# Pools at multiples of 2048 bytes, earlier modulation sums and later sums of activations in a two-layer encoder

## The chip, the cores and the metric

The kernel runs on one core of one Trainium2 chip. The metric is the device time of one launch in microseconds, as the median of several runs. The core has five engines with a queue of instructions each: TensorE (PE, matmuls; PEld is its weight loads), VectorE (DVE), ScalarE (ACT), GpSimd (POOL) and SyncE (SP, which issues the transfers). They wait for each other by semaphores. On-chip memory has 128 partitions; an address below is a byte offset within a partition.

## The reference, cut to what matters

A trunk of two layers works on 256 tokens of 2048 features in float32. Each layer has an attention part (two kinds of heads with one input and one output projection) and an MLP; a conditioning vector gives six vectors per layer that scale, shift and gate.

```
cond = silu(c)
for l in range(2):
    mod = cond @ w_ada[l] + b_ada[l]                 # 2048 x 12288
    sh_a, sc_a, g_a, sh_m, sc_m, g_m = split(mod, 6)
    h = rmsnorm(x) * (1 + sc_a) + sh_a
    proj = h @ w_in[l]
    ...                                              # differential and latent attention
    x = x + g_a * (concat([out_a, out_b]) @ w_o[l])
    h = rmsnorm(x) * (1 + sc_m) + sh_m
    y = square(relu(h @ w_mlp_in[l])) @ w_mlp_out[l] # 2048 -> 8192 -> 2048
    x = x + g_m * y
return rmsnorm(x, final_norm_g)
```

## The kernel before

Every float32 operand is split in two parts: ACT rounds it (hi, line 157), DVE subtracts to get the rest (lo, line 160), and PE forms hi·hi, hi·lo and lo·hi. A weight block of 1 MB arrives in a tile `raw` of a ring of five (pool wp, which also holds hi and lo); the same ring takes the blocks of w_ada. A modulation value costs one DVE instruction over 128x2048 (line 313, `ada`), one per block; each weight split adds a rate (RATE_A0 and so on) to a credit, and a credit of one loads the next block of w_ada, whose sum is put behind that split's last lo.

Layer 2's MLP (`mlp_last`) is the place of most of the change. The hidden features go in 32 pairs of 128-row blocks. `wides` multiplies two weight blocks by the normalized h into one bank: 16 matmuls of 512 columns (line 222, hi), then 16 of 256 columns (line 225, lo). `hidden` makes relu squared of a pair, its parts hidh and hidl (line 1390 is the DVE half), four sums of its quarters (lines 1100 to 1102, `sum4`) and the parts sumh and suml of these. The first three pairs were computed ahead, during the output projection; `leave` (that is `scaled`, line 657) takes them from their banks when the MLP begins. For the second matrix product a step either takes eight products of blocks (`eight`, operands hi and lo) or seven products with sums of weight blocks (`seven_weights`: u is formed by DVE on lines 1128 to 1130, parts dh, dl of the raw blocks and uh, ul of the sums on lines 1138 and 1139). `product` (lines 1147 to 1149) is three matmuls of 512 columns whose moving operand is the weight part. A seven-step is 9 matmuls on d and 12 on u; its third product reads the sums (sumh, suml), as do three of those on u. 42 of the 56 steps are seven-steps: 30 of them in the first half of the output (28 in the loop over pairs, two behind it) and 12 in the second, where the hidden parts are fetched back from memory (`back`).

In the loop pair j is computed while step j - 4 is multiplied. PE's order there is written out by hand: wides, products 1, 2, 3 (on d), wides, products 5, 7, 6, 4 (on u). Below, A to I are the wides in turn from the MLP's start, and S0, S1, S2 the first three seven-steps: PE's order is A, B, C, first products of S0, D, rest of S0, E, first products of S1, F, rest of S1, G, first products of S2, H, and so on. The order on DVE, ACT and SP comes from a scheduler, which has only the program and its own costs.

Pools are laid out one behind the other. In this kernel the tiles of the pools wp (hi, lo, raw, u), up and tp begin 512 bytes past a multiple of 2048, x 416 past one, and the last pools, kp among them (dh, dl, uh, ul), 1376 past one, which is 32 past a multiple of 64. dh, dl, uh, ul have one buffer each.

Of the kernel before, what the change touches and what calls it, by code (L numbers as in the profile page):

```python
# [10 lines left out]
F32 = mybir.dt.float32  # L11
F32R = mybir.dt.float32r
# [5 lines left out]
P = 128  # L18
T = 256
TX = T + 2  # L20
D = 2048
NK = D // P
# [31 lines left out]
V_LAM = 208  # L54
V_T = 216
V_C = 248
NVEC = 264


def two_pi_parts():  # L60
# [35 lines left out]
NAHEAD = 6  # L96
# [6 lines left out]

LATE = 2
TURNED = 0, 0, 2
RATE_A0, RATE_Q, RATE_A3, RATE_O, RATE_A1, RATE_A2, RATE_K, RATE_M, RATE_V = 0.7, 2.7, 1.7, 0.75, 0.5, 0.7, 0.6, 0.68, 1.15
FILL = "0|1|2|3|e|l||r"


class Trunk:  # L110
    def __init__(self, ctx, tc, io):
        self.nc, self.tc, self.io = tc.nc, tc, io
        pool = lambda name, bufs, **k: ctx.enter_context(tc.tile_pool(name=name, bufs=bufs, **k))
        self.fp = pool("fp", 1)
        self.wp = pool("wp", 4)
        self.up = pool("up", 40)
        self.tp = pool("tp", 6)
        self.cp = pool("cp", 1)
        self.sp = pool("sp", 8)
        self.pp = pool("pp", 8, space=bass.MemoryType.PSUM)  # L120
        self.late = ctx.enter_context(ExitStack())
        self.lp = self.late.enter_context(tc.tile_pool(name="lp", bufs=1))
        self.ap = self.late.enter_context(tc.tile_pool(name="ap", bufs=6))
        self.ada_todo, self.ada_here, self.rate, self.credit = [], [], 0.0, 0.0
        self.n = 0
        self.rt = []
        self.evict = None
        self.most = None
        self.hold = None
# [159 lines left out]
    def ada_plan(self):  # L289
        self.mod, self.macc = {}, {}  # L290
        for l in range(DEPTH):
            for g in range(6):
                self.mod[l, g] = self.cp.tile([P, NK], F32, name=f"mod{l}{g}")
                self.macc[l, g] = (self.cp if l else self.fp).tile([P, NK], F32, name=f"macc{l}{g}")
        for l in range(DEPTH):
            for gs in ((0, 1), (2,), (3, 4), (5,)):
                self.ada_todo += [(l, g, 2 * q + i) for q in range(8) for g in gs for i in range(2)]
        self.ada_todo.remove(TURNED)
# [55 lines left out]
    def setup(self):  # L354
        nc, io, cp = self.nc, self.io, self.cp
        self.ada_plan()
        self.cond = self.lp.tile([P, D], F32, name="cond")
        row = self.wp.tile([1, D], F32, tag="raw", name="c_row", bufs=5)
        nc.sync.dma_start(row, io["c"])
        tab = cp.tile([P, T + 8 + NCONST + NVEC], F32, name="tab")  # L360
        nc.scalar.dma_start(tab, io["tab"])
        self.pos = tab[:, : T + 8].bitcast(I32)
        self.K = tab[:, T + 8 : T + 8 + NCONST]
        self.vec = tab[:, T + 8 + NCONST :]
        self.x = cp.tile([P, NK, T], F32, name="x")
        for q in range(4):
            nc.sync.dma_start(self.x[:, 4 * q : 4 * q + 4], io["xT"][:, 4 * q : 4 * q + 4])
        self.mean = {}
        for n in (D, 2 * P):
            self.mean[n] = cp.tile([P, P], F32, name=f"mean{n}")  # L370
            nc.gpsimd.memset(self.mean[n], 1.0 / n)
        self.eps = cp.tile([P, 1], F32, name="eps")
        nc.gpsimd.memset(self.eps, EPS)
        self.ident = cp.tile([P, P], F32, name="ident")
        make_identity(nc, self.ident)
        self.ccol = cp.tile([P, NK], F32, name="ccol")
        self.lead = nc.scalar.activation(self.s("warm", 1), self.eps, AF.Silu)
        leads = []
        for j in range(4):
            c = slice(512 * j, 512 * j + 512)  # L380
            ps = self.bank("pc").rearrange("p a b -> p (a b)")
            nc.tensor.matmul(ps, self.mean[D][:1], row[:, c], start=True, stop=True)
            self.lead = nc.scalar.activation(self.cond[:, c], ps, AF.Silu, scale=float(D))
            leads.append(self.lead)
            if j == 0:
                self.bias_setup()
        nc.scalar.activation(self.ccol, self.vec[:, V_C : V_C + NK], AF.Silu)
        self.rel = {0: self.distances(0)}
        ps = self.bank("pn")[:, 0]
        for k in range(0, NK, 2):  # L390
            t = self.t("sqx")
            last = nc.scalar.activation(t, self.x[:, k : k + 2], AF.Square)  # L392
            self.follow(last, leads[min(3, 1 + k // 4)])
            for i in range(2):
                nc.tensor.matmul(ps, self.mean[D], t[:, i], start=k + i == 0, stop=k + i == NK - 1)
        self.follow(nc.scalar.activation(self.s("warm", 1), self.eps, AF.Sqrt), last)
        r = self.cp.tile([P, T], F32, tag="rstd", name="rstd", bufs=2)
        nc.scalar.activation(r, ps, AF.Sqrt, bias=self.eps)
        return r
# [6 lines left out]
    def lambdas(self):  # L406
        nc = self.nc
        e = self.s("lam_e", 4)
        v = self.vec[:, V_LAM : V_LAM + 8]
        nc.vector.tensor_tensor(v[:, :4], v[:, :4], v[:, 4:], ALU.mult)  # L410
        ps = self.bank("pl")[:, 0, :4]
        nc.tensor.matmul(ps, self.mean[D], v[:, :4], start=True, stop=True)
        nc.scalar.activation(e, ps, AF.Exp, scale=float(D))
        self.lam = self.cp.tile([P, 2], F32, name="lam")
        self.gl = self.cp.tile([P, 2, 2], F32, name="gl")
        for l in range(2):
            init = 0.8 - 0.6 * math.exp(-0.3 * l)
            nc.vector.scalar_tensor_tensor(
                self.lam[:, l : l + 1], e[:, 2 * l : 2 * l + 1], init, e[:, 2 * l + 1 : 2 * l + 2],
                ALU.add, ALU.subtract,  # L420
            )
            nc.vector.tensor_scalar(
                self.gl[:, l], self.vec[:, V_SUBLN + 2 * l : V_SUBLN + 2 * l + 2], 1.0 - init, None, ALU.mult
            )
# [319 lines left out]
    def layer(self, l, acc, st):  # L744
        nc, io = self.nc, self.io
# [12 lines left out]
        if l == 0:  # L758
            early = {p: next_by_k(kqs) for p, kqs in EARLY.items()}
# [4 lines left out]
        else:  # L764
            h = acc
            lat = []
            for b in range(0, NAHEAD, 2):
                t, c = self.scaled(st, b, self.u("cr"))
# [164 lines left out]
        with self.tc.manual_schedule(engines={mybir.EngineType.PE}) if l else nullcontext():  # L933
# [19 lines left out]
            self.rate = 0.0 if st else RATE_K  # L953
            if st:
                h = self.ahead_rest(st, 0, acc, 2, 5)
                first = NAHEAD, lambda: [self.scaled(st, b, self.t("sum")) for b in range(0, NAHEAD, 2)]
            else:
                h, banks = self.norm_then_by_k(l, acc, 3, 4, io["w_n0"], 3, 0)
                high = self.high
                first = NNORM, lambda: [  # L960
                    self.relu2(b, after=a) for b, a in zip(banks, [high, *self.highs, *self.highs[1:] * 3])
                ]
# [52 lines left out]
    def mlp_last(self, l, h, first, g):  # L1015
# [8 lines left out]
        lead = done // 2  # L1024
        banks = None

        def both(j, v, bias=None):
            hid[j], part[j] = self.hidden(v, bias)
            kept[j] = self.spill(hid[j], f"a{j}")
            if j in sevens:  # L1030
                kept[j] += self.spill(part[j], f"s{j}")

        for j in range(lead, NPAIR):
            pre = [self.t("pre") for _ in range(2)]
            step = j - LAG
            for i in range(2):
                (ps,) = self.wides([io["w_m1"][l, 2 * j + i - done]], h)
                if j == lead and i == 0:
                    for k, (v, c) in enumerate(leave()):
                        both(k, v, c)  # L1040
                for k in range(2):
                    self.nc.scalar.activation(pre[k][:, i], ps[:, k], AF.Copy)  # L1042
                if i:
                    self.nc.vector.tensor_tensor(pre[0], pre[0], pre[1], ALU.add)
                    both(j, pre[0])
                if step < 0:
                    continue
                if i == 0:
                    banks = banks or {p: self.flat(self.bank("p7")) for p in ORDER}
                    w = self.seven_weights(io["w_s"][0, step])  # L1050
                self.products(banks, ORDER[3:] if i else ORDER[:3], w, hid[step], part[step], step == 0)
# [16 lines left out]
        hid = []  # L1068
# [19 lines left out]
    def hidden(self, v, bias=None):  # L1088
# [6 lines left out]
            for i in range(2):  # L1095
                nc.scalar.activation(r[:, i], v[:, i], AF.Relu, bias=bias[:, i : i + 1])
        nc.scalar.activation(r, r, AF.Square)
        a = self.both(r, self.u("hidl", F32R), "hidh")
        s = self.t("sum4").rearrange("p a (b c) -> p (a b) c", c=P)
        nc.vector.tensor_tensor(s[:, 0:2], r[:, 0].rearrange("p (b c) -> p b c", c=P), r[:, :, P:], ALU.subtract)  # L1100
        nc.vector.tensor_tensor(s[:, 2], s[:, 1], r[:, 0, :P], ALU.subtract)
        nc.vector.tensor_tensor(s[:, 3], s[:, 2], r[:, 1, :P], ALU.add)
        return a, self.both(s.rearrange("p (a b) c -> p a (b c)", a=2), self.u("suml", F32R), "sumh")

    def spill(self, parts, name):
        out = []
# [84 lines left out]
    def end_plan(self, y, g):  # L1191
# [1 line left out]
        nc = self.nc  # L1193
        flat = self.flat
        self.gb, self.fgb = {}, {}
        self.part = self.cp.tile([P, 4, 2], F32, name="part")

        def rows_of(c):
            def f():
# [375 lines left out]
def _layout(i):  # L1575
# [13 lines left out]
    vec += [np.stack([f[f"diff_lambda_{a}{j}"][l] for a in "qk" for l in range(2) for j in (1, 2)], 1)]  # L1589
    vec += [np.repeat(f["rel_bias_table"].reshape(8, 4, HD).transpose(1, 0, 2).reshape(4, 32), 32, 0)]  # L1590
    vec += [feat(f["c"][0], NK)]
    a["tab"] = np.concatenate([pos.view(np.float32), consts()] + vec, 1)
    assert a["tab"].shape == (P, T + 8 + NCONST + NVEC)
    a["fg"] = np.ascontiguousarray(np.broadcast_to(f["final_norm_g"], (P, D)))
# [60 lines left out]
```

## Time and profile before

| | |
|---|---|
| median of 3 runs | 2167.95 us (2166.28 to 2168.47) |
| the profiled execution, its own time | 2167.24 us |
| its span on the core | 2165.5 us |
| PE busy | 2136.4 us, 99% |
| DVE busy | 1822.7 us, 84% |
| ACT busy | 1231.3 us, 57% |
| bytes moved | 632.58 MB, mean 292 GB/s |

The span runs from the first to the last recorded instruction; 1.7 us of the execution's time lie around it. The busy share of an engine is an average over stages. Matmuls overlap: one of 512 columns is recorded with 0.39 us or more while the next starts some 0.23 us later, so the pace is read from the starts. "PEclk" is the granted share of full TensorE clock in a stretch.

### The profile page before, as it was taken

The numbers are of one execution on the slowest core, as the hardware profiler recorded it, in microseconds if no ns is written. First come the engines' busy times: TensorE is split into PE (matmuls) and PEld (weight loads), VectorE is DVE, ScalarE is ACT, GpSimd is POOL, SyncE is SP. The second block draws the span as 40 slices with busy tenths as digits, with TensorE's granted clock in tenths as the row PEclk, the third lists the DMA queues.
The fourth block names the chain that finished last, engine by engine and source line by source line (L and its number), as shares of the span: only waits on it lengthen the run. The fifth ranks groups of instructions, "written<-read, shape, count | busy, mean of one in ns | idle before, by whom it ended". The sixth has DMA issues, their size and how long they took to land. (4 is left out here: it accounts for less than half of the span.)

```text
span 2165.5 us, 30890 instructions
## 1 busy us (share of the span) xinstructions
PE 2136.4 (99%) x11922; PEld 1867.1 (86%) x11922; DVE 1822.7 (84%) x2362; ACT 1231.3 (57%) x1893; POOL 22.6 (1%) x43
## 2 busy tenths in 40 slices
PE   9999999999999999999999999998999999999998
PEld 7899888998888888888889898998888888887887
DVE  8999888897778778778788878799888888888877
ACT  6565664464464355355456665647766666665554
POOL 0000000000000000000001000000000000000000
PEclk9999999999999999999999999999999999999999
DMA  9987988799888889888867648685766766658983
GB/s 400 423 337 265 348 312 300 263 372 347 317 306 339 327 306 339 319 315 318 319 230 275 253 165 296 243 309 199 286 262 228 262 239 235 261 211 315 358 330 155
DMA packets 110885, 632.58 MB, mean 292 GB/s; under 512 B 12305, under 2 KB 12305, under 8 KB 44689
## 3 DMA queue, kind: packets, MB, share of 16 engines
q1 hardware_dynamic: 110450, 629.99, 77.7%
q8 instruction: 93, 1.52, 0.3%
q10 hardware_dynamic: 288, 0.62, 0.1%
q14 instruction: 54, 0.44, 0.1%
HBM read 605.40 MB, written 25.17 MB: 291 GB/s over the span
## 5 line engine op out<-in xcount | busy, mean ns | idle before, releaser
L160 DVE TENSOR_TENSOR lo<-raw,hi 128x1024 fp32r<-128x1024 f32 (+1 forms) x636 | 745.0, 1191 | 218.3 <-ACT hi L157 147.6
L157 ACT ACTIVATE hi<-raw 128x1024 fp32r<-128x1024 f32 (+1 forms) x636 | 643.9, 1032 | 452.6 <-PE py L1303 189.7
L222 PE MATMUL ps<-h,hi 128*128 128x512 f32 x2016 | 477.9, 392 | 0.0
L222 PEld LDWEIGHTS ps<-h,hi 128*128 128x128 f32 x2016 | 377.6, 188 | 79.9 <-ACT hi L157 0.6
L313 DVE SCALAR_TENSOR_TENSOR ada<-ada,cond 128x2048 f32<-128x2048 f32 x191 | 435.2, 2284 | 2.5 <-ACT sqx L392 1.5
L225 PEld LDWEIGHTS ps<-h,lo 128*128 128x128 f32 x2016 | 254.7, 192 | 9.6 <-DVE lo L160 2.5
L225 PE MATMUL ps<-h,lo 128*128 128x256 f32 x2016 | 257.4, 283 | 1.9 <-DVE lo L160 1.9
L1299 PE MATMUL py<-hi,hid 128*128 128x512 f32 x512 | 163.1, 389 | 0.0
L1301 PE MATMUL py<-lo,hid 128*128 128x512 f32 x512 | 163.0, 389 | 0.0
L1303 PE MATMUL py<-hi,hid 128*128 128x512 f32 x512 | 162.9, 389 | 0.0
L1301 PEld LDWEIGHTS py<-lo,hid 128*128 128x128 f32 x512 | 96.1, 188 | 20.3 <-DVE lo L160 0.4
L1303 PEld LDWEIGHTS py<-hi,hid 128*128 128x128 f32 x512 | 96.1, 188 | 19.9
L1299 PEld LDWEIGHTS py<-hi,hid 128*128 128x128 f32 x512 | 95.8, 188 | 19.6
L1139 DVE TENSOR_TENSOR ul<-u,uh 128x2048 fp32r<-128x2048 f32 x42 | 96.3, 2292 | 17.7 <-ACT uh L1138 15.0
L1138 ACT ACTIVATE dh<-raw 128x1024 fp32r<-128x1024 f32 x84 | 66.5, 839 | 74.3 <-PE p L1149 39.5
L1042 ACT ACTIVATE pre<-ps 128x256 f32<-128x256 f32 x116 | 38.2, 380 | 110.3 <-PE ps L225 110.3
L1138 ACT ACTIVATE uh<-u 128x1024 fp32r<-128x1024 f32 x84 | 88.3, 1057 | 20.8 <-issue 12.3
L198 PE MATMUL pk<-h,hi 128*128 128x256 f32 x304 | 85.6, 288 | 1.5 <-ACT h L670 1.5
L200 PE MATMUL pk<-h,lo 128*128 128x256 f32 x304 | 85.9, 286 | 1.0 <-DVE lo L160 1.0
L199 PE MATMUL pk<-h,hi 128*128 128x256 f32 x304 | 86.4, 286 | 0.1
L1139 DVE TENSOR_TENSOR dl<-raw,dh 128x1536 fp32r<-128x1536 f32 x42 | 73.6, 1754 | 5.5 <-ACT dh L1138 5.5
L252 PE MATMUL pk<-hf,w 128*128 128x256 f32 x288 | 63.2, 379 | 0.2 <-ACT hf L675 0.2
(383 smaller groups left out, 3823.9 us busy)
## 6 DMA issues: line engine op xcount, KB each, us to landing
ada<-in_w_ada SPq DMA_DIRECT2D x191, 1024.0 KB, 5.2
raw<-in_w_m SPq DMA_DIRECT2D x174, 1024.0 KB, 5.7
raw<-in_w_s SPq DMA_DIRECT2D x56, 1024.0 KB, 6.5
raw<-in_w_ob SPq DMA_DIRECT2D x24, 1024.0 KB, 4.9
raw<-in_w_dv SPq DMA_DIRECT2D x16, 1024.0 KB, 4.8
raw<-in_w_q SPq DMA_DIRECT2D x16, 1024.0 KB, 4.8
back<-a SPq DMA_DIRECT2D x64, 256.0 KB, 6.3
raw<-in_w_n SPq DMA_DIRECT2D x16, 768.0 KB, 6.0
```

Of the source, the lines that this page charges most:

```text
L157: ins = self.high = nc.scalar.activation(hi, v, AF.Copy)
L160: ins = nc.vector.tensor_tensor(lo, v, hi.bitcast(F32), ALU.subtract)
L199: mm(ps, hi, x[1], start=False, stop=False, skip_group_check=shared)
L200: mm(ps, lo, x[0], start=False, stop=last, skip_group_check=shared)
L222: mm(ps.rearrange("p a b -> p (a b)"), part(w, 0, k), both, start=k == 0, stop=False)
L225: mm(ps[:, 0], part(w, 1, k), x, start=False, stop=k == nk - 1)
L313: ins = nc.vector.scalar_tensor_tensor(w, w, 1.0, self.cond, ALU.mult, ALU.mult, accum_out=acc[:, i : i + 1])
L1138: nc.scalar.activation(hi[:, c:m], v[:, c:m], AF.Copy)
L1139: nc.vector.tensor_tensor(lo, v, hi.bitcast(F32), ALU.subtract)
L1299: mm(o, xh[:, tok], hi[:, part[j]], start=start, stop=False)
L1301: mm(o, xh[:, tok], lo[:, part[j]], start=False, stop=False)
L1303: mm(o, xl[:, tok], hi[:, part[j]], start=False, stop=stop)
```

## The change

Three things change. First, the layout: small tiles move into the first pool, a table gets 62 columns of zeros, and a tile "gap" fills up to the last pools, so that the pools wp, up, tp and kp, the tile x and the first of the tiles of the attention's pools begin at multiples of 2048. Second, RATE_A2, the rate at which blocks of w_ada are loaded in the second layer's output projection, goes from 0.7 to 0.78. Third, the sums of the first three pairs are no longer formed in one go when these pairs leave their banks, but each at the first wides of its step; their tiles therefore live in pool up and not in tp.

```diff
-NVEC = 264
+NVEC = 326
...
-RATE_A0, RATE_Q, RATE_A3, RATE_O, RATE_A1, RATE_A2, RATE_K, RATE_M, RATE_V = 0.7, 2.7, 1.7, 0.75, 0.5, 0.7, 0.6, 0.68, 1.15
+RATE_A0, RATE_Q, RATE_A3, RATE_O, RATE_A1, RATE_A2, RATE_K, RATE_M, RATE_V = 0.7, 2.7, 1.7, 0.75, 0.5, 0.78, 0.6, 0.68, 1.15
...
         self.pp = pool("pp", 8, space=bass.MemoryType.PSUM)
+        pool("gap", 1).tile([P, 64], F32, name="gap")
         self.late = ctx.enter_context(ExitStack())
...
+        self.x = self.cp.tile([P, NK, T], F32, name="x")
+        self.mean = {n: self.cp.tile([P, P], F32, name=f"mean{n}") for n in (D, 2 * P)}
+        self.ident = self.cp.tile([P, P], F32, name="ident")
+        self.ccol = self.fp.tile([P, NK], F32, name="ccol")
+        self.eps = self.fp.tile([P, NK], F32, name="eps")[:, :1]
...
+        self.fp.tile([P, 24], F32, name="rest")
...
-                first = NAHEAD, lambda: [self.scaled(st, b, self.t("sum")) for b in range(0, NAHEAD, 2)]
+                first = NAHEAD, lambda: [self.scaled(st, b, self.u("sum")) for b in range(0, NAHEAD, 2)]
...
-        def both(j, v, bias=None):
-            hid[j], part[j] = self.hidden(v, bias)
+        def own(j, v, bias=None):
+            hid[j] = self.hidden(v, bias)
             kept[j] = self.spill(hid[j], f"a{j}")
+
+        def sums(j, v):
+            part[j] = self.sums4(v)
             if j in sevens:
                 kept[j] += self.spill(part[j], f"s{j}")
...
                 if j == lead and i == 0:
-                    for k, (v, c) in enumerate(leave()):
-                        both(k, v, c)
+                    early = [own(k, v, c) or v for k, (v, c) in enumerate(leave())]
...
                 if i:
                     self.nc.vector.tensor_tensor(pre[0], pre[0], pre[1], ALU.add)
-                    both(j, pre[0])
+                    own(j, pre[0])
+                    sums(j, pre[0])
                 if step < 0:
                     continue
                 if i == 0:
+                    if step < lead:
+                        sums(step, early[step])
                     banks = banks or {p: self.flat(self.bank("p7")) for p in ORDER}
                     w = self.seven_weights(io["w_s"][0, step])
...
-        a = self.both(r, self.u("hidl", F32R), "hidh")
+        return self.both(r, self.u("hidl", F32R), "hidh")
+
+    def sums4(self, r):
+
+        nc = self.nc
         s = self.t("sum4").rearrange("p a (b c) -> p (a b) c", c=P)
...
-        return a, self.both(s.rearrange("p a (b c) -> p a (b c)", a=2), self.u("suml", F32R), "sumh")
+        return self.both(s.rearrange("p (a b) c -> p a (b c)", a=2), self.u("suml", F32R), "sumh")
```

The order of PE and of POOL is the same in both kernels. DVE, ACT and SP differ from the second layer's output projection on. Three places on DVE matter below; the lines of the changed kernel stand some ten further down (160 is 170, 1100 to 1102 are 1111 to 1113, 1139 is 1150, 1390 is 1400).

The first place is where the MLP begins. `lo` of raw_2462 belongs to wides A, `h` is the normalized input and `mod15` the last gate values. In the kernel before:

```order
L671 SCALAR_TENSOR_TENSOR h_2456_14005<-ht_2455_14004,mod13_100,h_2456_14005 128x256
L671 SCALAR_TENSOR_TENSOR h_2457_14006<-ht_2455_14004,mod13_100,h_2457_14006 128x256
L313 SCALAR_TENSOR_TENSOR ada_2458_14016,macc15_105<-ada_2458_14016,cond_106 128x2048
L160 TENSOR_TENSOR lo_2464_14033<-raw_2462_14030,hi_2463_14032 128x1024
L326 TENSOR_TENSOR mod15_104<-macc15_105,tab_109 128x2
L160 TENSOR_TENSOR lo_2466_14037<-raw_2462_14030,hi_2465_14036 128x1024
```

And in the changed kernel:

```order
L673 SCALAR_TENSOR_TENSOR h_2455_14007<-ht_2453_14005,mod13_114,h_2455_14007 128x256
L673 SCALAR_TENSOR_TENSOR h_2457_14015<-ht_2456_14014,mod13_114,h_2457_14015 128x256
L673 SCALAR_TENSOR_TENSOR h_2458_14016<-ht_2456_14014,mod13_114,h_2458_14016 128x256
L170 TENSOR_TENSOR lo_2464_14039<-raw_2462_14036,hi_2463_14038 128x1024
L170 TENSOR_TENSOR lo_2466_14043<-raw_2462_14036,hi_2465_14042 128x1024
L659 TENSOR_TENSOR sum_2467_14078<-pa_2375_13520,rstd_2404_13699 128x256
```

The modulation sum between h and lo is gone from here; it and the one before it stand earlier, in the output projection and among the first h.

The second place is step S0: dl and ul are the parts of its weights, `sum4` of raw `sum_2467` and its `suml_2499` belong to pair 0, which S0's third product reads. The next two lo are those of wides D. In the kernel before, where pair 0's suml stood 16 rows further up:

```order
L1139 TENSOR_TENSOR dl_2517_14282<-raw_2514_14275,dh_2516_14281 128x1536
L1130 TENSOR_TENSOR u_2515_14277<-u_2515_14277,raw_2514_14275 128x512
L1139 TENSOR_TENSOR ul_2519_14287<-u_2515_14277,uh_2518_14286 128x2048
L160 TENSOR_TENSOR lo_2523_14304<-raw_2521_14301,hi_2522_14303 128x1024
L160 TENSOR_TENSOR lo_2525_14308<-raw_2521_14301,hi_2524_14307 128x1024
```

And in the changed kernel:

```order
L1150 TENSOR_TENSOR dl_2511_14268<-raw_2508_14261,dh_2510_14267 128x1536
L1113 TENSOR_TENSOR sum4_2487_14187<-sum4_2487_14187,pre_2459_14033 128x128
L1111 TENSOR_TENSOR sum4_2498_14246<-sum_2467_14078 128x256
L1150 TENSOR_TENSOR ul_2513_14273<-u_2509_14263,uh_2512_14272 128x2048
L1400 TENSOR_TENSOR suml_2488_14191<-sum4_2487_14187,sumh_2489_14192 128x512
L1112 TENSOR_TENSOR sum4_2498_14246<-sum4_2498_14246,sum_2467_14078 128x128
L170 TENSOR_TENSOR lo_2517_14290<-raw_2515_14287,hi_2516_14289 128x1024
L1113 TENSOR_TENSOR sum4_2498_14246<-sum4_2498_14246,sum_2467_14078 128x128
L170 TENSOR_TENSOR lo_2519_14294<-raw_2515_14287,hi_2518_14293 128x1024
L1400 TENSOR_TENSOR suml_2499_14250<-sum4_2498_14246,sumh_2500_14251 128x512
```

suml of pair 0 now stands behind ul of S0 and both lo of D.

The third place is step S1: `ul_2541` is the part of its u, `suml_2534` that of pair 1, which its third product reads, `raw_2556` the weights of wides G and `u_2565` the sums of S2's weights. In the kernel before pair 1's suml stood before dl of S0, and behind ul of S1 came:

```order
L1139 TENSOR_TENSOR ul_2544_14435<-u_2540_14425,uh_2543_14434 128x2048
L1390 TENSOR_TENSOR suml_2529_14356<-sum4_2528_14352,sumh_2530_14357 128x512
L160 TENSOR_TENSOR lo_2550_14456<-raw_2546_14449,hi_2549_14455 128x1024
L160 TENSOR_TENSOR lo_2561_14534<-raw_2559_14531,hi_2560_14533 128x1024
L160 TENSOR_TENSOR lo_2563_14538<-raw_2559_14531,hi_2562_14537 128x1024
L1128 TENSOR_TENSOR u_2565_14577<-raw_2564_14575 128x1024
```

And in the changed kernel, directly behind ul of S1:

```order
L1400 TENSOR_TENSOR hidl_2520_14334<-pre_2490_14199,hidh_2521_14335 128x512
L1111 TENSOR_TENSOR sum4_2522_14342<-pre_2490_14199 128x256
L170 TENSOR_TENSOR lo_2558_14532<-raw_2556_14529,hi_2557_14531 128x1024
L1112 TENSOR_TENSOR sum4_2522_14342<-sum4_2522_14342,pre_2490_14199 128x128
L1111 TENSOR_TENSOR sum4_2533_14409<-sum_2469_14084 128x256
L1113 TENSOR_TENSOR sum4_2522_14342<-sum4_2522_14342,pre_2490_14199 128x128
L1112 TENSOR_TENSOR sum4_2533_14409<-sum4_2533_14409,sum_2469_14084 128x128
L170 TENSOR_TENSOR lo_2560_14536<-raw_2556_14529,hi_2559_14535 128x1024
L1400 TENSOR_TENSOR suml_2523_14346<-sum4_2522_14342,sumh_2524_14347 128x512
L1113 TENSOR_TENSOR sum4_2533_14409<-sum4_2533_14409,sum_2469_14084 128x128
L1139 TENSOR_TENSOR u_2565_14583<-raw_2564_14581 128x1024
L1400 TENSOR_TENSOR suml_2534_14413<-sum4_2533_14409,sumh_2535_14414 128x512
```

suml of pair 1 stands twelve instructions behind ul of S1. That of pair 2 stands in the same way behind ul of S2, with suml, a sum, a lo, a sum, a lo, a sum and two parts of u between them.

## Rows read from the trace of the kernel before

**Rows 1.** Page, part 1: busy us (share of the span), instructions of each engine.
```profile
PE 2136.4 (99%) x11922; PEld 1867.1 (86%) x11922; DVE 1822.7 (84%) x2362; ACT 1231.3 (57%) x1893; POOL 22.6 (1%) x43
```

**Rows 2.** Windows: length, busy PE, PEld, DVE, ACT, POOL (instructions), PEclk, DMA share, GB/s.
```profile
1460.00:1480.00 20.00, 20.00 (x170) 20.00 (x169) 17.22 (x34) 14.30 (x27) 3.16 (x8) 1.00 0.62 206
...
1496.00:1499.60 3.60, 3.60 (x14) 3.10 (x14) 3.60 (x10) 3.60 (x8) 0.00 (x0) 0.53 0.03 7
...
1513.30:1520.00 6.70, 4.85 (x11) 3.51 (x12) 5.58 (x5) 3.07 (x4) 0.00 (x0) 0.50 0.96 350
1520.00:1536.00 16.00, 16.00 (x86) 13.73 (x86) 14.22 (x17) 12.55 (x18) 0.00 (x0) 1.00 0.75 294
```

**Rows 3.** Timeline of PE at the MLP's start: start us, us, instruction, count, [idle before].
```profile
1489.26 3.84 PE L222 MATMUL ps<-h,hi 128*128 128x512 f32 x16
1495.01 3.28 PE L225 MATMUL ps<-h,lo 128*128 128x256 f32 x16 [1.92 <-DVE lo L160]
...
1502.46 2.08 PE L225 MATMUL ps<-h,lo 128*128 128x256 f32 x16
...
1509.94 0.39 PE L1147 MATMUL p<-dh,hidh 128*128 128x512 f32 x1
1515.15 0.79 PE L1148 MATMUL p<-dl,hidh 128*128 128x512 f32 x1 [4.82 <-DVE dl L1139]
...
1518.78 4.55 PE L222 MATMUL ps<-h,hi 128*128 128x512 f32 x16
...
1527.87 3.82 PE L222 MATMUL ps<-h,hi 128*128 128x512 f32 x16
...
1533.44 0.39 PE L1147 MATMUL p<-dh,hidh 128*128 128x512 f32 x1
...
1535.30 0.39 PE L1149 MATMUL p<-dh,suml 128*128 128x512 f32 x1
...
1551.55 3.82 PE L222 MATMUL ps<-h,hi 128*128 128x512 f32 x16
```

**Rows 4.** Timeline of PE in the second half, products of 512 columns.
```profile
1990.87 0.50 PE L1148 MATMUL p<-ul,back 128*128 128x512 f32 x1 [1.71 <-DVE ul L1139]
...
1999.02 0.40 PE L1147 MATMUL p<-dh,back 128*128 128x512 f32 x1
...
2001.14 0.39 PE L1147 MATMUL p<-uh,back 128*128 128x512 f32 x1
...
2003.94 0.40 PE L1147 MATMUL p<-hi,back 128*128 128x512 f32 x1
...
2006.70 0.39 PE L1147 MATMUL p<-hi,back 128*128 128x512 f32 x1
...
2009.42 0.40 PE L1147 MATMUL p<-dh,back 128*128 128x512 f32 x1
```

**Rows 5.** Timeline of DVE at the MLP's start.
```profile
1491.52 2.29 DVE L313 SCALAR_TENSOR_TENSOR ada<-ada,cond 128x2048 f32<-128x2048 f32 x1
...
1493.73 1.23 DVE L160 TENSOR_TENSOR lo<-raw,hi 128x1024 fp32r<-128x1024 f32 x1
...
1500.67 0.70 DVE L1390 TENSOR_TENSOR hidl<-sum,hidh 128x512 fp32r<-128x512 f32 x1
1501.27 0.29 DVE L1101 TENSOR_TENSOR sum<-sum,sum 128x128 f32<-128x128 f32 x1
1501.47 0.43 DVE L1100 TENSOR_TENSOR sum<-sum 128x256 f32<-128x256 f32 x1
...
1511.01 1.22 DVE L1128 TENSOR_TENSOR u<-raw 128x1024 f32<-128x1024 f32 x1
...
1513.35 1.75 DVE L1139 TENSOR_TENSOR dl<-raw,dh 128x1536 fp32r<-128x1536 f32 x1
...
1516.82 2.29 DVE L1139 TENSOR_TENSOR ul<-u,uh 128x2048 fp32r<-128x2048 f32 x1 [1.12 <-ACT uh L1138]
```

**Rows 6.** Timeline of ACT at step S0.
```profile
1515.74 1.06 ACT L1138 ACTIVATE uh<-u 128x1024 fp32r<-128x1024 f32 x1 [2.42 <-DVE u L1130]
```

More of the change, by code (lines that the diff above doesn't have):

```diff
@@ L123, in __init__ @@
         self.ap = self.late.enter_context(tc.tile_pool(name="ap", bufs=6))
+        self.x = self.cp.tile([P, NK, T], F32, name="x")
[3 more added lines that the diff above has]
+        self.eps = self.fp.tile([P, NK], F32, name="eps")[:, :1]
+        self.lam = self.fp.tile([P, NK], F32, name="lam")[:, :2]
+        self.gl = self.fp.tile([P, NK], F32, name="gl")[:, :4].rearrange("p (a b) -> p a b", b=2)
+        self.part = self.fp.tile([P, 4, 2], F32, name="part")
+        self.fp.tile([P, 24], F32, name="rest")
         self.ada_todo, self.ada_here, self.rate, self.credit = [], [], 0.0, 0.0
@@ L292, in ada_plan @@
             for g in range(6):
-                self.mod[l, g] = self.cp.tile([P, NK], F32, name=f"mod{l}{g}")
-                self.macc[l, g] = (self.cp if l else self.fp).tile([P, NK], F32, name=f"macc{l}{g}")
+                self.mod[l, g] = self.fp.tile([P, NK], F32, name=f"mod{l}{g}")
+                self.macc[l, g] = self.fp.tile([P, NK], F32, name=f"macc{l}{g}")
         for l in range(DEPTH):
@@ L364, in setup @@
         self.vec = tab[:, T + 8 + NCONST :]
-        self.x = cp.tile([P, NK, T], F32, name="x")
         for q in range(4):
             nc.sync.dma_start(self.x[:, 4 * q : 4 * q + 4], io["xT"][:, 4 * q : 4 * q + 4])
-        self.mean = {}
         for n in (D, 2 * P):
-            self.mean[n] = cp.tile([P, P], F32, name=f"mean{n}")
             nc.gpsimd.memset(self.mean[n], 1.0 / n)
-        self.eps = cp.tile([P, 1], F32, name="eps")
         nc.gpsimd.memset(self.eps, EPS)
-        self.ident = cp.tile([P, P], F32, name="ident")
         make_identity(nc, self.ident)
-        self.ccol = cp.tile([P, NK], F32, name="ccol")
         self.lead = nc.scalar.activation(self.s("warm", 1), self.eps, AF.Silu)
@@ L413, in lambdas @@
         nc.scalar.activation(e, ps, AF.Exp, scale=float(D))
-        self.lam = self.cp.tile([P, 2], F32, name="lam")
-        self.gl = self.cp.tile([P, 2, 2], F32, name="gl")
         for l in range(2):
@@ L1102, in hidden @@
         nc.vector.tensor_tensor(s[:, 3], s[:, 2], r[:, 1, :P], ALU.add)
-        return a, self.both(s.rearrange("p (a b) c -> p a (b c)", a=2), self.u("suml", F32R), "sumh")
+        return self.both(s.rearrange("p (a b) c -> p a (b c)", a=2), self.u("suml", F32R), "sumh")
     def spill(self, parts, name):
@@ L1195, in end_plan @@
         self.gb, self.fgb = {}, {}
-        self.part = self.cp.tile([P, 4, 2], F32, name="part")
         def rows_of(c):
@@ L1591, in _layout @@
     vec += [feat(f["c"][0], NK)]
+    vec += [np.zeros((P, NVEC - V_C - NK), np.float32)]
     a["tab"] = np.concatenate([pos.view(np.float32), consts()] + vec, 1)
```

## The prediction

> **What bounds the kernel now.** I read the engines' busy shares first: PE 99%, DVE 84%, ACT 57% [rows 1]. A share that high leaves two ways to gain: PE's pace, and the few microseconds in which PE stands or runs at half clock. So I read the pace from PE's timeline in a long stretch without gaps, then looked for gaps in the stretch that the change rewrites, the start of the second MLP.
>
> Pace: in the second half, matmuls of 512 columns with moving operands hi or lo settle at (2009.42 - 2006.70) / 12 = 226.7 ns from start to start; those with uh or ul run at (2003.94 - 2001.14) / 12 = 233.3 ns, and those with dh or dl at (2001.14 - 1999.02) / 9 = 235.6 ns [rows 4]. Shape, stationary operand (`back`) and PSUM are alike. In the loop the d products run at (1535.30 - 1533.44) / 8 = 232.5 ns [rows 3].
>
> Gaps: wides A waits 1.92 us for lo, which DVE makes behind a modulation sum of 2.29 us; S0's second matmul waits 4.82 us for dl [rows 3, 5]. [...] One wides takes 1533.44 - 1527.87 = 5.57 us at full clock [rows 3]. From 1495.01 to the start of 1502.46 the work is one wides plus the same place, 5.57 us, and took 7.45: 1.9 us lost. Behind the second gap eight products took 1518.78 - 1515.15 = 3.63 us instead of 1.86, and D to E took 9.09 us instead of 5.57 + 12 x 0.233 = 8.37: 1.8 + 0.7 us lost [rows 3]. In all the beginning loses 1.9 + 1.9 + 4.8 + 2.5 = 11.1 us.
>
> **Part 1, the addresses.** dh, dl, uh and ul move from 1376 past a multiple of 2048 to 0. hi and lo start at 512 past and keep the best pace, so what I hold against 1376 is that it is 32 past a multiple of 64. If the four then run like hi and lo: u, 42 x 12 = 504 matmuls by 6.6 ns, 3.3 us; d in the first half, 30 x 9 = 270 by 5.8 ns, 1.6 us; d in the second, 12 x 9 = 108 by 8.9 ns, 1.0 us. Sum 5.9 us, all on the path, since PE does not stand there. Ends: 0 if the address is not the cause; 7.5 us if what runs behind them settles sooner as well (the 12 matmuls from 2003.94 took 2.76 us, not 2.72 [rows 4]; 0.04 us at some 40 changes of operand). I take 5.9, which is what the rows give directly.
>
> [...]
>
> For DVE and ACT I take nothing: dl at 1376 takes 1.75 us for 1536 columns, 1.14 ns each, the sum at 512 takes 2.29 for 2048, 1.12 [rows 5]. The 62 columns of zeros add 32 KB to one load at the start, beside blocks of 1 MB; nothing. That `sum` tiles come from another pool costs no instruction.
>
> **Part 2, the two modulation sums.** They are not saved, only earlier: 2.2 us of DVE each and a load of 1 MB, in the output projection, where DVE has 2.8 us free of 20 and PE does not stand [rows 2]. If that cover is gone, one sum in front of a lo costs at most its 2.2 us, once. At the MLP's start lo of A begins when h ends, at 1491.52 in place of 1493.73 [rows 5], and is there at 1492.7; PE needs it after A's sixteen matmuls of 512 columns, at about 1492.9. The gap of 1.92 us and its 1.9 us of half clock go. What is late next is dl of S0.
>
> **Part 3, the sums.** I walk DVE from 1491.52, from start to start (0.09 us less than the durations): lo 1.14, parts of 512 columns 0.60, sums of 256 and 128 columns 0.34 and 0.20, u 1.13, dl 1.67, ul 2.20 [rows 5]. Up to dl stand six lo (A, B, C), six scaled sums at 0.34, four hidl, pre and two parts of u (seven at 0.60), u, two sums and dl: 6.8 + 2.0 + 4.2 + 1.1 + 0.5 + 1.7 = 16.4 us, with one wait of half a microsecond for ACT ready at 1508.4. PE reaches S0 at 1489.26 + 3 x 5.57 = 1506.0 and waits 2.2 us for dl, not 4.8. But the third product now needs pair 0's suml, and behind dl stand sums 0.20 and 0.34, ul 2.20, suml 0.60, sum 0.20, lo 1.14, sum 0.20, lo 1.14, suml 0.60: 6.6 us. It comes at 1515.0 where the matmuls from dl on need 1.8 us, so PE waits 4.8 us more, and D begins at 1515.3, not 1518.78: 3.5 us gained.
>
> Step S1. Call T the end of S0 (1527.87 before). PE needs pair 1's suml at T + 7.43 (1535.30 - 1527.87) [rows 3]. It stands behind ul of S1, which needs uh, whose single buffer is free only at T: two ACT instructions of 1.06 [rows 6], so T + 2.1. From ul to the end of suml: ul 2.20, hidl 0.60, sum 0.34, lo 1.14, sums 0.20, 0.34, 0.20, 0.20, lo 1.14, suml 0.60, sum 0.20, u 1.13, suml 0.60: 8.9 us, so T + 11.0. PE waits 3.6 us. Behind the waiting matmul stand F and all that follows.
>
> Step S2. The end T2 of S1 is T + 11.2 + 8.4. DVE reaches ul of S2 before that, uh is there at T2 + 2.1, and up to pair 2's suml stand ul, suml, sum, lo, sum, lo, sum, two parts of u, suml: 7.6 us, T2 + 9.7, against T2 + 7.43: 2.3 us. From S3 on the sums are formed four pairs ahead, as before, and DVE is busy 14.2 of 16 us in a step [rows 2].
>
> Clock. Two of the old stretches cost 1.9 and 2.5 us. S0's stays, in the new waits; whether the waits of 3.6 and 2.3 us bring stretches of their own is open: nothing (the gap of 1.71 us at 1990.87 was followed by products at 0.23 us [rows 4]) to 2 x 2.6 us. I take one, 2.6, since 1.92 us did it at A.
>
> So wides H, at 1551.55 before [rows 3], starts at 1551.55 - 3.5 + 3.6 + 2.3 + 2.6 = 1556.5: the beginning loses 5.0 us. Ends: -3.5 if only S0 waits, +9 with both stretches and D at half clock for longer. The gap at 1990.87 keeps its order of work, a lo more or less, 1 us either way; no term.
>
> **Sum.** Against the profiled execution: 2167.24 (span 2165.5) - 5.9 + 5.0 = 2166.3. The median of the runs is 0.7 above that execution, so 2167.0 beside 2167.95. A difference under 0.2%, 4.3 us, can't be told from no change here.
>
> **Rivals.**
> A: the sums bind only at S0. For it: S0's wait is shorter by what DVE no longer does first, and DVE has slack in a step; against it, the order puts pair 1's suml twelve instructions behind an ul that can't start before T. The beginning then gains 3.5 us: 2167.95 - 3.5 - 5.9 = 2158.5.
> [...]
> C: as forecast, but each new wait brings its stretch at half clock: the beginning loses 9, so 2167.95 + 9 - 5.9 = 2171.
> [...]
>
> **Chances and range.** Forecast 0.50, with 3.5 us on either side (2163.5 to 2170.5); A 0.27; B 0.11; C 0.12. Faster by over 0.2%: A, and a fifth of the forecast's own spread, 0.36. Slower: B, half of C and a little of the forecast, 0.22. Within: 0.42. The range 2158 to 2173 leaves out about half of A, half of B and a tail of C, 2 in 10.
>
> **What would show it.** Right: in the changed trace products on d and u settle at 227 ns in the second half; wides A runs into its lo without a gap; S0 waits first for dl (2 us) and then at its third product for suml (5 us); S1 and S2 wait for suml at the third matmul of product 3 (3.6 and 2.3 us), with a PEclk near 0.5 somewhere behind. Wrong: 233 ns as before (then 2173), or S1 and S2 without a wait (then 2158), or a DMA that holds D or F back, which I have not priced.

## The result and the profile after

The changed kernel takes 2175.59 us (median of 8 runs, 2172.36 to 2177.32) against 2167.03 for the kernel before beside it: ratio 1.0039, 95% interval 1.0028 to 1.0050. That is 8.6 us slower, outside the forecast range of 2158 to 2173. The profiled execution took 2176.97 us (span 2175.2), 9.7 more than that of before and 1.4 above the median of its own runs.

PE is as busy as before in microseconds; the share fell because the span grew. Page, part 1 (answers to [rows 1]):

```profile
PE 2138.1 (98%) x11922; PEld 1872.2 (86%) x11922; DVE 1816.0 (83%) x2362; ACT 1244.7 (57%) x1893; POOL 18.5 (1%) x43
```

What PE waited for from the MLP's start to the second half of its output, after the change (engine and line, releaser: us, times, longest):

```profile
PE p L1158 <- ACT sumh L1399: 10.0, 3, 3.6
PE p L1158 <- ACT uh L1149: 3.9, 1, 3.9
PE p L1159 <- DVE dl L1150: 1.8, 1, 1.8
```

Before, this stretch had 4.8 us for dl, 1.9 for lo and 1.7 for ul [rows 3, 4]. Three waits for sums are new, and one wait of 3.9 us at the start of the second half that nobody expected. PE's timeline (answers to [rows 3]):

```profile
1490.77 3.80 PE L232 MATMUL ps<-h,hi 128*128 128x512 f32 x16
1494.41 2.08 PE L235 MATMUL ps<-h,lo 128*128 128x256 f32 x16
...
1509.64 0.50 PE L1159 MATMUL p<-dl,hidh 128*128 128x512 f32 x1 [1.78 <-DVE dl L1150]
...
1515.18 0.80 PE L1158 MATMUL p<-dh,sumh 128*128 128x512 f32 x1 [3.37 <-ACT sumh L1399]
...
1516.85 5.42 PE L232 MATMUL ps<-h,hi 128*128 128x512 f32 x16
...
1526.77 3.79 PE L232 MATMUL ps<-h,hi 128*128 128x512 f32 x16
...
1537.49 0.79 PE L1158 MATMUL p<-dh,sumh 128*128 128x512 f32 x1 [3.64 <-ACT sumh L1399]
...
1538.57 0.80 PE L1160 MATMUL p<-dh,suml 128*128 128x512 f32 x1
1539.16 4.59 PE L232 MATMUL ps<-h,hi 128*128 128x512 f32 x16
...
1548.25 3.79 PE L232 MATMUL ps<-h,hi 128*128 128x512 f32 x16
...
1558.35 0.79 PE L1158 MATMUL p<-dh,sumh 128*128 128x512 f32 x1 [3.01 <-ACT sumh L1399]
...
1559.62 0.79 PE L1160 MATMUL p<-dh,suml 128*128 128x512 f32 x1
1560.21 5.90 PE L232 MATMUL ps<-h,hi 128*128 128x512 f32 x16
...
1567.85 0.40 PE L1158 MATMUL p<-uh,sumh 128*128 128x512 f32 x1
```

Wides A has lost its gap. D starts 1.9 us earlier than before, though A began 1.5 us later (1.3 of that a weight load that landed late in the output projection of this execution; of five other profiles at the new rate one shows 0.6 us there, four none). H starts 8.7 us later. In each of the three steps PE stands at the first matmul of product 3, which reads ACT's sumh, and the third, which reads suml, follows about a microsecond later. The windows show why each wait costs more than itself (columns as in [rows 2]):

```profile
1516.85:1520.50 3.65, 3.65 (x10) 2.85 (x9) 3.65 (x4) 1.58 (x2) 0.00 (x0) 0.53 1.02 428
...
1533.70:1537.49 3.79, 0.15 (x1) 0.00 (x1) 3.79 (x9) 1.26 (x2) 0.00 (x0) 0.98 0.89 302
1537.49:1541.00 3.51, 3.51 (x8) 2.49 (x9) 2.31 (x4) 1.57 (x2) 0.00 (x0) 0.53 0.65 198
...
1558.35:1564.00 5.65, 5.60 (x12) 3.96 (x13) 3.12 (x4) 1.72 (x3) 0.00 (x0) 0.50 0.61 251
...
1992.40:1998.40 6.00, 5.97 (x15) 4.71 (x16) 5.37 (x7) 0.00 (x0) 0.00 (x0) 0.52 1.05 405
```

Behind each of the three waits for sums, and behind the one in the second half, the granted clock stands at 0.50 to 0.53. During the wait of 1533.70 to 1537.49 DVE is busy all the time: it isn't waiting, it is doing other things first. At S0 the clock had fallen before the wait for the sums: the window from 1509.64 to 1511.60, right behind the wait of 1.78 us for dl, shows 0.60, and that from 1511.60 to 1515.18 shows 0.50.

The start of the second half, on PE, and the pace there (answers to [rows 4]):

```profile
1992.43 0.77 PE L1158 MATMUL p<-hi,back 128*128 128x512 f32 x1 [3.93 <-ACT uh L1149]
...
2010.85 0.39 PE L1158 MATMUL p<-dh,back 128*128 128x512 f32 x1
...
2012.89 0.39 PE L1158 MATMUL p<-uh,back 128*128 128x512 f32 x1
...
2015.61 0.39 PE L1158 MATMUL p<-hi,back 128*128 128x512 f32 x1
```

d runs at 2.04 / 9 = 226.7 ns, u at 2.72 / 12 = 226.7 ns: the pace of hi and lo. The queue of SP in front of that, after the change (start, time from the first issue to the last, DMAs, count):

```profile
1977.53 9.37 SPq L184 DMA_DIRECT2D raw<-in_w_s  x3
1986.95 2.17 SPq L1128 DMA_DIRECT2D back<-a  x4
```

and in the kernel before, where PE used the first fetch at 1981.18:

```profile
1964.62 8.58 SPq L174 DMA_DIRECT2D raw<-in_w_s  x3
1973.25 1.91 SPq L1117 DMA_DIRECT2D back<-a  x4
```

Before, the fetches left 7.9 us ahead of their use. Now they left at 1986.95 where PE wanted them at 1988.33, and landed 5.5 us after their issue (median of the first three). The last of the three weight loads ahead of them was issued at 1986.57, after SP had waited 4.3 us for a lo of DVE (line 170), and the first fetch followed it at 1986.95. Before, this load stood behind fourteen fetches and was issued at 1985.63.

The account, by starts of the same matmul in both profiles: +1.5 us at A; +10.7 when H's wides are done and S2's products on u begin (1567.85 against 1557.12); 3.6 us less by the pace up to the end of the first half (1988.33 against 1981.18 leaves 7.15); +5.0 at the start of the second half; 2.4 less by the pace in the second half; +9.7 at the end. The 5.0 are 4.1 us that PE stood from 1988.33 to 1992.43, and 2.7 us at the lower clock (0.52), since the first 24 products from there took 8.22 us instead of 5.48, less the 1.9 us that PE stood for ul before.

### The profile page after: what moved, and what is told of

It reads as the page before. It is cut to its first block, busy times and chain, and to the rows that moved or that the text cites. A ratio compares the mean times of both kernels' runs of the same rounds, so it can differ in the third digit from the quotient of the medians.

```text
span 2175.2 us, 30986 instructions
## 1 busy us (share of the span) xinstructions
PE 2138.1 (98%) x11922; PEld 1872.2 (86%) x11922; DVE 1816.0 (83%) x2362; ACT 1244.7 (57%) x1893; POOL 18.5 (1%) x43
## 4 chain that ended last, share of the span: by engine, by line
PE 90%; DVE 5%; ACT 2%; DMA 2%; issue 1%; DVEq 0%; ACTq 0%; SPq 0%
PE ps L232 24%; PE ps L235 12%; PE py L1311 6%; PE py L1309 6%; PE py L1313 6%; PE p L1158 4%; PE p L1160 4%; PE p L1159 4%; PE pk L262 3%; PE pv L277 2%; PE pv L278 2%; PE pk L208 2%; DVE lo L170 2%; PE pk L209 1%; PE pv L276 1%; PE pk L210 1%
## 5 line engine op out<-in xcount | busy, mean ns | idle before, releaser
L262 PEld LDWEIGHTS pk<-hf,w 128*128 128x128 f32 x288 | 54.5, 190 | 7.5
```

Source lines behind the costliest of these rows:

```text
L262: self.nc.tensor.matmul(ps, w[i][:, j * P : j * P + P], whole[i], start=first, stop=last, skip_group_check=True)
```

## The experiments

All ratios are against the kernel before on the same chip.

**The address alone, 32 bytes.** The order of all engines is that of the kernel before.

```diff
+        pool("gap", 1).tile([P, 8], F32, name="gap")
         self.late = ctx.enter_context(ExitStack())
```

> The kernel before with one more tile of 32 bytes per partition ahead of the last pools, so that dh, dl, uh, ul begin 1408 past a multiple of 2048 (a multiple of 64, not of 2048); the order of all engines is unchanged. Theory (32 past a multiple of 64 is what slows them): the products on d and u settle at 227 ns, 5 us faster, ratio 0.9977. Rival (only multiples of 2048 help, or the address is not the cause and the changed kernel's 227 ns came from its other order): they stay at 232 to 236 ns, ratio 1.000.

Measured: ratio 0.9995 (0.9986 to 1.0004), 2165.37 us. PE's timeline in the second half:

```profile
2001.95 0.40 PE L1148 MATMUL p<-dh,back 128*128 128x512 f32 x1
...
2004.04 0.39 PE L1148 MATMUL p<-uh,back 128*128 128x512 f32 x1
...
2006.84 0.39 PE L1148 MATMUL p<-hi,back 128*128 128x512 f32 x1
```

2.09 / 9 = 232.2 and 2.80 / 12 = 233.3 ns: at 1408, a multiple of 64, d and u don't reach 227 ns. My reading of the offset had failed, so the question was which offset counts.

**The layout of the change alone.** The changed kernel with the old rate, the old place of the sums and `sum` in pool tp; order as before.

```diff
-RATE_... = 0.7, 2.7, 1.7, 0.75, 0.5, 0.78, ...
+RATE_... = 0.7, 2.7, 1.7, 0.75, 0.5, 0.7, ...
-                first = NAHEAD, lambda: [self.scaled(st, b, self.u("sum")) for b in range(0, NAHEAD, 2)]
+                first = NAHEAD, lambda: [self.scaled(st, b, self.t("sum")) for b in range(0, NAHEAD, 2)]
...
-                    early = [own(k, v, c) or v for k, (v, c) in enumerate(leave())]
+                    for k, (v, c) in enumerate(leave()):
+                        own(k, v, c)
+                        sums(k, v)
...
-                    if step < lead:
-                        sums(step, early[step])
```

> Only the layout of the changed kernel, with the rate and the sums of the kernel before; the order of the engines is that of before. Theory: 227 ns and 5 us faster, ratio 0.9977, the same as with 32 bytes. Rival (the pools of hi, lo and of the hidden parts at multiples of 2048 count as well): clearly more than with 32 bytes, ratio 0.996 or less.

Measured: 0.9972 (0.9963 to 0.9982), 2160.88 us: 6.1 us faster by the ratio, the rows settling at 227 ns. Since the order is that of before, the address is the cause, and my 5.9 us were its size. That it would be the same as with 32 bytes, as I had expected, was wrong.

**The offset narrowed down.** 160, 672 and 416 bytes in place of 32, one execution each.

> The kernel before with 160 bytes ahead of the last pools: dh, dl, uh, ul begin 1536 past a multiple of 2048, a multiple of 512; hi, lo and the hidden parts stay at 512. Theory (a multiple of 512 is enough, as 512 is for hi and lo): d and u settle at 227 ns, the time falls by about 5 us. Rival (only a multiple of 2048, or the same offset as the hidden parts, helps): they stay at 232 to 235 ns.

> The kernel before with 672 bytes ahead of the last pools: dh, dl, uh, ul begin at a multiple of 2048, while the hidden parts stay 512 past one. Theory (the moving operand's own address decides): 227 ns, about 5 us faster. Rival (the offset against the stationary operand's pool decides): 232 ns or more.

> The kernel before with 416 bytes ahead of the last pools: dh, dl, uh, ul begin 1792 past a multiple of 2048, a multiple of 256 and not of 512. If multiples of 512 are what is wanted, the products stay at 232 ns or more; if 256 does, they settle at 227 ns.

All three reach the pace; with 416 bytes (1792 past a multiple of 2048):

```profile
2008.15 0.39 PE L1148 MATMUL p<-dh,back 128*128 128x512 f32 x1
...
2010.19 0.39 PE L1148 MATMUL p<-uh,back 128*128 128x512 f32 x1
...
2012.91 0.39 PE L1148 MATMUL p<-hi,back 128*128 128x512 f32 x1
```

2.04 / 9 and 2.72 / 12, 226.7 ns. The single times are 2161.95 (160 bytes), 2161.34 (672) and 2164.09 (416), beside medians of 2166 to 2167 before; a single execution is not enough to tell these apart. Offsets 0, 512, 1536 and 1792 run at 226.7 ns, 1376 and 1408 at 232 or more: here multiples of 256 were good and 1408, a multiple of 128, was not. The hidden parts' own offset stayed at 512 in these three runs, and d and u ran at 226.7 ns with theirs at 1536, 0 and 1792. Moving the last pools alone gives the pace that the whole new layout gives (226.7 ns).

**The rate alone.** 0.78 on the kernel before.

> Only the rate 0.78, on the kernel before. Theory: the gap of 1.9 us before lo of wides A and its stretch at half clock go (3 to 4 us), a wait of some 1.5 us for a weight load comes in the output projection, and S0 still waits for dl; in all 1 to 3 us faster, ratio 0.9985 to 0.9995, and no gap at the start of the second half. Rival (the loads moved by the rate are what costs the time, also at the start of the second half): slower, ratio 1.003 or more.

Measured: 0.9989 (0.9980 to 0.9998), 2164.85 us, no wait at the start of the second half but the old one for ul. The gap at wides A became two of 0.8 us at B and C, and S0 waits 3.4 us for dl. The ratio is as expected; the wait of some 1.5 us in the output projection that I had expected did not come. The rate is not the cause of the slower time.

**The sums at once again.** The changed kernel without the putting off (the last two hunks of the edit above; the rate 0.78 and the new place of the `sum` tiles stay).

> The changed kernel with the sums of the first three pairs formed in one go as before. Theory (the put-off sums cost the waits at S0, S1, S2, and move a weight load past the fetches at the start of the second half): no wait for sumh at S1 and S2, no gap of 4 us at the start of the second half, 6 to 8 us faster than the kernel before, ratio 0.9965. Rival (the rate or the layout is behind the gaps): they stay, ratio 1.002 or more.

Measured: 0.9964 (0.9951 to 0.9976), 2158.98 us. The same list of waits:

```profile
PE p L1159 <- DVE dl L1150: 3.4, 1, 3.4
PE p L1159 <- DVE ul L1150: 1.9, 1, 1.9
PE ps L235 <- DVE lo L170: 1.5, 2, 0.8
PE ps L232 <- ACT pre L1048: 0.7, 1, 0.7
```

No wait for sumh, none for uh: both losses are the put-off sums', 2175.59 - 2158.98 = 16.6 us in all, the later one too, 430 us behind the place of the edit. The two gaps of 0.7 and 0.8 us before lo are those of the rate alone, at B and C.

**The changed kernel at the old rate.** Layout and put-off sums.

> The changed kernel with the old rate 0.7: layout and put-off sums alone. Theory: the weight load still stands ahead of the fetches on SP, so the wait of some 4 us at the start of the second half stays; the wait before lo of wides A (1.9 us) is back; S1 still waits some 2 us, since pair 1's suml stands eight instructions behind ul. Slower than the changed kernel with the sums at once (2159) by 5 to 10 us: ratio 0.999 to 1.002. Rival (the sums wait only because the rate moved DVE's work): no wait at S1 and S2 and no gap in the second half, ratio 0.997.

Measured: 1.0037 (1.0023 to 1.0050), 2173.89 us; I had expected 1.002 at most, with 2 us at S1, where PE waited 4.5. The waits for sums are as large (10.2 us for sumh and 1.3 for suml), so the rate neither causes nor softens them. In this profile the releaser at the start of the second half is named directly:

```profile
PE p L1158 <- DMA back<-a: 3.6, 1, 3.6
```

**The order on SP.** The changed kernel, with the weight load of the second half's fifth step ordered behind the first two fetches.

```diff
-        self.nc.sync.dma_start(raw, src)
+        ins = self.nc.sync.dma_start(raw, src)
+        if getattr(self, "raw_after", None) is not None:
+            self.follow(ins, self.raw_after)
+            self.raw_after = None
...
             a = self.fetch(kept[j][:2])
+            if j == 0:
+                fetched = self.fetched
+            if j == 4:
+                self.raw_after = fetched
...
-            self.nc.sync.dma_start(v.bitcast(F32), d)
+            self.fetched = self.nc.sync.dma_start(v.bitcast(F32), d)
```

> The changed kernel with one order added on SP: the weight load of the second half's fifth step is issued behind the first two fetches of hidden parts, not ahead of them. Theory (that load waits for its ring buffer until DVE has used it, and the fetches stand behind it): the wait of 3.9 us at the start of the second half and its half-clock stretch go, some 5 us faster than the changed kernel, ratio to the kernel before about 1.0015; the waits at S0, S1, S2 stay at 3.4, 3.6 and 3.0 us. Rival (the wait is ACT's uh or the freeing of a bank, as the profile's releaser says): it stays, ratio 1.004.

Measured: 1.0015 (1.0006 to 1.0024), 2170.41 us, 5.2 us less than the changed kernel. The waits from the MLP's start on:

```profile
PE p L1165 <- ACT sumh L1406: 10.8, 3, 4.1
PE p L1166 <- DVE dl L1157: 1.8, 1, 1.8
PE p L1166 <- DVE ul L1157: 1.6, 1, 1.6
PE p L1167 <- DVE suml L1407: 0.5, 1, 0.5
```

The waits for sums stay (S0's is 4.1 us here, not 3.4), that of 3.9 us is gone and the old one for ul is back. So the releaser "ACT uh" of the changed kernel's list was only the last event before; the cause was the fetch.

**The sums half a step earlier.** The changed kernel, each early pair's sums behind the second wides of the step before.

```diff
                     sums(j, pre[0])
+                if i and 0 <= step + 1 < lead:
+                    sums(step + 1, early[step + 1])
...
-                    if step < lead:
-                        sums(step, early[step])
```

> The changed kernel with the sums of each early pair formed half a step earlier (at the second wides of the step before its own). Theory (what counts is how many DVE instructions stand between ul and suml): pair 1's suml now stands two subtractions behind suml of pair 4, at T + 6.7 us by the same walk against T + 7.4 needed, so no wait at S1 and S2, and at S0 some 1.5 us in place of 3.4; and the load on SP stands behind the fetches again, so no wait at the start of the second half: as fast as the changed kernel with the sums formed at once, ratio 0.9955 to 0.997. Rival (any putting off costs, since DVE has no slack there): waits at S1 and S2 stay, ratio 1.000 or more.

Measured: 0.9961 (0.9948 to 0.9973), 2159.09 us. Waits:

```profile
PE p L1159 <- DVE dl L1150: 2.7, 1, 2.7
PE p L1160 <- DVE suml L1400: 1.6, 2, 0.9
PE p L1159 <- DVE ul L1150: 1.4, 1, 1.4
```

S1 waits no longer; S0 waits 0.9 us for suml and S2 0.7. In time this is not told apart from the sums at once, so putting off as such costs nothing that shows here; by half a step too much it cost 16 us.

**dl before u.** The same kernel, with the three sums of `seven_weights` behind dl.

> As the run with the sums half a step earlier, and in the weights of a seven-step dl is made before the sums u. Theory (what is late at S0 is dl, behind three sums of u and other work of DVE): dl of S0 is there before PE needs it, S0 then waits some 2 us for suml and not 2.7 for dl; 2 to 4 us faster than 2159, ratio 0.9945 to 0.9955. Rival (ACT's dh or the weight load is what comes last): the wait for dl stays and the ratio is 0.996.

Measured: 0.9962 (0.9948 to 0.9975), 2157.4 us; not told apart from the run before in time, and less than expected. The wait for dl is gone; in its place:

```profile
PE p L1161 <- DVE suml L1401: 2.0, 2, 1.3
PE p L1159 <- ACT sumh L1400: 1.3, 1, 1.3
PE p L1159 <- DMA back<-a: 0.9, 1, 0.9
PE p L1160 <- DVE ul L1151: 0.8, 1, 0.8
```

It and its two neighbours (the sums half a step earlier, the sums at once) are 8 to 9 us faster than the kernel before and 16 to 18 faster than the changed one.

## Why the prediction was wrong

Part 1 held in size, not in reason. 5.9 us were forecast; the layout alone gave 6.1 (3.9 to 8.0 by its interval). That 1376 is 32 past a multiple of 64 doesn't explain it: d took 235.6 ns there [rows 4] and still 232.2 at 1408, a multiple of 64, against 226.7 at 1792. Rival B (the address isn't the cause, so part 1 gives 0 and the time is 2167.95 + 5.0 = 2173.0) fell with the runs of 160, 672 and 416 bytes: in these kernels, which differ from the one before by the gap tile alone, d and u ran at 226.7 ns.

In the profiles of before and after, the pace gave 3.6 and 2.4 us behind the beginning, 6.0 in all.

Part 2 held: the gap at A went, and from A to C 11.1 us went by instead of 15.1. The rate alone gave 0.9989 where the gain at A was to be 3.8 us, since part of it came back as the gaps at B and C (12.2 us from A to C). A itself came 1.5 us late in the profiled execution, for which the forecast had no term.

Part 3 named the right place and was too small. Its walk held at S0: from the end of dl to the end of pair 0's suml 6.6 us went by (6.6 forecast), and D began 3.4 us earlier than before, counted from A (3.5 forecast). At S1 and S2 it did not hold. DVE's rows, and ACT's at S1:

```profile
1529.53 2.29 DVE L1150 TENSOR_TENSOR ul<-u,uh 128x2048 fp32r<-128x2048 f32 x1 [2.44 <-ACT uh L1149]
...
1537.83 0.69 DVE L1400 TENSOR_TENSOR suml<-sum,sumh 128x512 fp32r<-128x512 f32 x1
...
1551.73 2.28 DVE L1150 TENSOR_TENSOR ul<-u,uh 128x2048 fp32r<-128x2048 f32 x1
...
1558.88 0.69 DVE L1400 TENSOR_TENSOR suml<-sum,sumh 128x512 fp32r<-128x512 f32 x1
```

```profile
1527.93 0.61 ACT L1100 ACTIVATE pre<-pre 128x512 f32<-128x512 f32 x1
1528.45 1.04 ACT L1149 ACTIVATE uh<-u 128x1024 fp32r<-128x1024 f32 x1
```

From ul's start to the end of suml 9.0 us went by at S1 (8.9 forecast) and 7.8 at S2 (7.6): that part was right. The third matmul of product 3 started 0.05 us behind the end of suml in both steps (1538.57 and 1559.62), so up to there the sums set the time. It was due 7.43 us behind T and T2 and came 11.8 and 11.4 us behind them: 4.4 and 3.9 us late, where 3.6 and 2.3 were forecast. The list's 3.6 us at S1 agree with the forecast by chance: they end with ACT's sumh, at the first matmul of the product, which the walk had left out.

Three steps of the prediction failed. The first is "two ACT instructions of 1.06, so T + 2.1". ul started at T + 2.8 and T2 + 3.5. At S1 ACT put a relu of a newer pair (`pre`, 1527.93) between the two halves of uh; at S2 ACT began uh only at T2 + 0.75 and put hidh between its halves, and DVE too was busy up to T2 + 3.5. That made the sums 0.8 and 1.6 us later than forecast.

The second is the term for the clock: "I take one, 2.6". All three waits were followed by a stretch with the granted clock at 0.50 to 0.53. From D to E 9.92 us went by instead of 8.29 at the new pace, 0.8 more than the 9.09 of before. Behind the third matmul of S1, 0.59 us passed to F instead of 0.23, and 9.09 from F to G instead of 8.29: 1.2 us. Behind that of S2, 0.59 passed to H, and H took 7.64 instead of 5.57: 2.4 us. The two new stretches cost 3.6 us where one of 2.6 was taken, and S0's 0.8 more than before.

From A to the end of H the change lost 10.7 - 1.5 = 9.2 us where 5.0 were forecast; of the 4.2 between them, 2.4 are the later sums and 1.8 the clock. Rival C's 9 us for the beginning came out in size, but only in part for its reason.

The third is "keeps its order of work, a lo more or less, 1 us either way; no term". I had walked DVE to the start of the second half and not SP, though SP's order differs too. One weight load stood there ahead of fourteen fetches instead of behind them, waited for its ring buffer, and the fetches waited with it. That was 5.0 us net in the profiles, 5.2 in time when undone. The prediction had named a DMA as a possible sign of being wrong, but at D and F, and without a price.

The sum: -6.0 for the pace, +9.2 at the beginning, +5.0 in the second half, +1.5 at A: 9.7 us, as the profiles differ. Without the 4.2 us at the beginning, or without the 5.0 in the second half, the time would have been inside the range, at about 2171.

What stays open: why the scheduler puts that load ahead when the sums are late; which property of an offset counts below 256 bytes, and whether every multiple of 256 is good (four were run); and whether the two remaining waits of the fastest runs, 1 to 3 us each, can be had.

## What to carry to other kernels

When work is put off to "its step", count what stands ahead of it on its engine at that step and compare with the time at which PE asks for it: half a step decided between 8 us faster and 8 us slower. The walk has to take in the other engine's instructions too: here ACT's uh and sumh came later than a walk along DVE alone gave. Walk every queue whose order differs, the DMA queue first, over the whole rest of the program: here one load that waited 4.3 us on SP held back the fetches behind it, and ordering it behind the first two of them gave 5.2 us. In the changed kernel each of the four waits of 3.0 to 3.9 us on PE was followed by a stretch at a granted clock of 0.50 to 0.53 that cost another 1.2 to 2.7 us; price it each time, not once.

## What the runs showed of the hardware

A matmul of 512 float32 columns ran at 226.7 ns from start to start when its moving operand began at 0, 512, 1536 or 1792 past a multiple of 2048 bytes (changed kernel, hi and lo before, 160 and 416 bytes), and at 232 to 236 ns at 1376 or 1408 (before, 32 bytes). VectorE showed nothing of this: dl took 1.75 us with its tiles at 1376 [rows 5] and at 0 (from 1507.83 in the changed kernel) alike. In the changed kernel waits of PE from 3.0 to 3.9 us were each followed by windows of 3.5 to 6 us with the granted clock at 0.50 to 0.53. That of 1.92 us at wides A before was followed by 0.53, that of 4.82 us at S0 before by 0.50 [rows 2, 3], and that of 1.78 us at S0 after the change by 0.60 and then 0.50; that of 1.71 us at 1990.87 before was not (1.00 from 1992 on) [rows 4].
